# One decoder layer on one core: a product's two half-tiles closed in one step, a gated chunk turned two steps later

## The chip, the cores and the metric

The kernel runs on one core of a Trainium2 chip. The metric is the device time of one execution in microseconds (us), lower is better. Five engines work side by side, each through its own queue in order: TensorE (PE; PEld is its weight load), VectorE (DVE), ScalarE (ACT), GpSimd (POOL), and SyncE (SP), which here issues nearly all DMAs. An instruction that waits holds up all that stands behind it on its engine.

## The reference

One layer over 512 tokens of width 2048, all in float32:

```python
h = rms_norm(x, norm1_g)
qa, ka, va, ra, ga, qb, kb, vb = split(h @ w_in)        # combined projection
out_a = gla_mixer(qa, ka, va, ra, log_g(ga), onorm_g)   # gated linear attention, 4 heads
                                                        # ends with rms_norm(o) * silu(ra)
out_b = dilated_mixer(rms(qb), rms(kb), vb, rel_bias)   # 8 heads
x = x + concat(out_a, out_b) @ w_out                    # "the output product"
h2 = rms_norm(x, norm2_g)
x = x + (silu(h2 @ w_gate) * (h2 @ w_up)) @ w_down      # hidden width 5632
```

## The kernel before

**Products.** Every large matrix product is done in pairs of 512 output columns by a seven-product scheme (`P1 P5 P6 P3 P7 P2 P4`) instead of eight block products. The activations are operands in `apool` (tiles `AA` for single blocks, `AS` for sums of blocks), the weights stream in as quarters `wa wb wc wd` of 512 KB. One *item* is one product times one of four row groups: ACT casts the weight tile to a high part `wh` (L320), DVE takes the low part `wl` (L324, and first a sum of two quarters at L230 where the product needs one), and PE runs 8 matmuls with `wh` and 4 with `wl` (L364). `stream` writes the items of all pairs out one after the other; `wh` and `wl` have two buffers each.

**Side work.** After the eighth matmul of each item `p.step()` runs. It counts down every entry of `later(units, fn)` by one and emits those that reach zero; so `later(2, ...)` means two items on. Then it emits some of the `background` jobs. All this is only the order of the program: a scheduler then sets each engine's own order from it, by its own costs, and places the waits.

**Closing.** Four products close an output chunk: `P3` closes (half 0, which 1), `P7` (1,1), `P2` (0,0), `P4` (1,0). `half` is a half of the tokens, `which` one of the pair's two chunks of 512 columns. `close` adds the product (two PSUM tiles `acc`, m = 0 and 1) to the two `seed` tiles on DVE, m = 0 one step after the product's end (L277), m = 1 two steps after it, and then calls `final`.

**The output product** is two pairs: columns 0 to 1023, then 1024 to 2047 (`final_out(1)`). There `final` adds the residual (`seed<-seed,q` and `seed<-seed,k`, L1445), stores the rows to `x_d`, sums their squares (ACT L1478), scales them (ACT L1453, tile `L`), and two steps later PE turns them by 8 transposes (L1166, `bank<-mats,L`); ACT copies the banks out (L1177, tiles `oT` and `PT`) and SP stores them to `xn_d`, from where the operands of the feed-forward product are loaded. For (1,1) `final` also queues `early_jobs` and `late_jobs`: the first load both token halves of `xn_d[6]` and `xn_d[7]` into tiles `top` (L1227), cast them (ACT L178, DVE L179, `AA<-top`) and form the difference of the two halves (DVE L1265) with its cast `AS<-top`. The chunk closed by (1,1) is one of these halves.

**The gate rows.** The pair before the output product makes `r`; `final_gate` multiplies the attention output by silu(r), tile `cr` in its last call, which takes `P4`'s PSUM directly (`src is acc_`). `rest` (L1215) finishes the product and queues `transposed_store`, which turns the two tiles by 8 transposes (`bank<-mats,cr`), copies them out (ACT L1174, `turned`) and stores them to `mix_d`, from where later `late_jobs` load them for the sums `late<-oT,late` (DVE L1300). Tiles called `C`, which hold `seed` and `cr`, have six buffers; PSUM tiles `bank` have four.

Of the kernel before, what the change touches and what calls it, by code (L numbers as in the profile page):

```python
# [31 lines left out]
PRODUCTS = ("P1", "P5", "P6", "P3", "P7", "P2", "P4")  # L32
# [76 lines left out]
def block_kernel(ctx: ExitStack, tc: tile.TileContext, ins, out):  # L109
# [19 lines left out]
    def nm(s):  # L129
        uid[0] += 1  # L130
        return f"{s}_{uid[0]}"
# [4 lines left out]
    def bank():  # L136
        return ps.tile([P, 512], F32, name=nm("bank"), tag="bank")

    def work(tag, shape=(P, 512), bufs=1):
        return mp.tile(list(shape), F32, name=nm(tag), tag=tag, bufs=bufs)  # L140
# [25 lines left out]
    class Operand:  # L166


        def __init__(self, groups):
            self.groups = groups  # L170
            self.t = {}
# [20 lines left out]
    def unfolded(t):  # L192

        return t.rearrange("p (a b) -> p b a", b=2)

    def halves(t):
        return t.rearrange("p (b a) -> p b a", b=2)

    class Pair:


        def __init__(
            self, op, rows, w1, w2, final, step, scale=None, before=None, products=PRODUCTS
        ):
            self.op, self.rows, self.w1, self.w2 = op, rows, w1, w2
            self.final, self.step, self.scale, self.before = final, step, scale, before
            self.q, self.dst, self.held = {}, {}, {}
            self.products = products
            self.closes = {**CLOSES}
            if products is FIRST_CLOSED:  # L210
                self.closes["P1"] = self.closes.pop("P2")
# [62 lines left out]
        def close(self, seed, src, half, which):  # L274
            def one(m):
                if self.scale is None:
                    nc.vector.tensor_tensor(  # L277
                        halves(seed[m]), unfolded(src[m]), halves(seed[m]), op=ALU.add
                    )
                else:  # L280
                    nc.vector.scalar_tensor_tensor(  # L281
                        halves(seed[m]), unfolded(src[m]), self.scale(half, m), halves(seed[m]),
                        op0=ALU.mult, op1=ALU.add,
                    )
                if m == 1:
                    self.final(half, which, seed, None)

            later(1, lambda: one(0))
            later(2, lambda: one(1))

        def end(self, prod):
            src = self.dst[prod]
# [84 lines left out]
    def soon(fn, groups=1):  # L377

        soonest.append([groups, fn])
# [123 lines left out]
    def later(units, fn, hold=False):  # L503

        deferred.append([units, fn, hold])
# [49 lines left out]
    def rate(*stretches):  # L555


        owed = [0.0]
        rates = iter([r for n, r in stretches for _ in range(n)])

        def go():
            owed[0] += next(rates, stretches[-1][1])
            n = owed[0] if owed[0] > 0.3 else 0
            owed[0] = min(owed[0] - (step(n) or 0.0), 1.0)

        return go
# [592 lines left out]
    def transposed_store(tiles, half, dsts, gains=None, spare=None):  # L1159

        for b in range(2):
            bk = bank().rearrange("p (j n) -> p j n", j=2)
            for jj in range(2):
                for m in range(2):
                    f = (2 * b + jj) * P
                    nc.tensor.transpose(  # L1166
                        bk[:, jj, m * P : (m + 1) * P], tiles[m][:, f : f + P], ident
                    )
            if spare is None:
                d = work(("oT", "PT")[b], (P, 2, 256))  # L1170
            else:
                d = spare[:, b]
            if gains is None:
                nc.scalar.copy(d, bk)  # L1174
            else:
                for jj in range(2):
                    nc.scalar.activation(  # L1177
                        d[:, jj, :], bk[:, jj, :], AF.Copy,
                        scale=gains[:, 2 * b + jj : 2 * b + jj + 1],
                    )  # L1180
            store(dsts[b][:, :, half * 256 : (half + 1) * 256], d)
            done.add((id(dsts[b]), half))
# [9 lines left out]
    def final_gate(half, which, tiles, acc_):  # L1192
        og = onorm.pop((half, which))
        if tiles is None:
            tiles = [cpool.tile([P, 512], F32, name=nm("cr"), tag="C") for _ in range(2)]
            src = acc_
        else:
            src = tiles
        for m in range(2):
            if src is acc_:  # L1200
                nc.vector.scalar_tensor_tensor(
                    halves(og[m]), unfolded(src[m]), row_scale(half, m), halves(og[m]),
                    op0=ALU.mult, op1=ALU.mult,
                )
                neg = nrs1[:, 2 * half + m : 2 * half + m + 1]
                nc.scalar.activation(halves(tiles[m]), unfolded(src[m]), AF.Exp, scale=neg)
            else:
                nc.vector.tensor_tensor(og[m], src[m], og[m], op=ALU.mult)
                nc.scalar.activation(tiles[m], src[m], AF.Exp, scale=-1.0)
            nc.scalar.activation(tiles[m], tiles[m], AF.Ln, bias=1.0)  # L1210
            nc.scalar.activation(tiles[m], tiles[m], AF.Exp, scale=-1.0)

        def rest():
            for m in range(2):
                nc.vector.tensor_tensor(tiles[m], tiles[m], og[m], op=ALU.mult)  # L1215
            spare = apool.tile([P, 2, 2, 256], F32, name=nm("turned"), tag="A")
            later(3 - (src is acc_), lambda: transposed_store(
                tiles, half, mix_d[2 * which : 2 * which + 2], spare=spare
            ))

        soon(rest, 2)
# [174 lines left out]
    opm = Operand(4)  # L1396
# [5 lines left out]
    def pair(*args, **kw):  # L1402
        pairs.append(Pair(*args, **kw))

    pair(opx, rows_in, col(1536), col(1024), final_proj("va1", "va0"), rate((22, 1), (6, 0.6)),
         row_scale, before=lambda: background.extend([gates(), bias_tables()]))
# [5 lines left out]
         products=FIRST_CLOSED)  # L1412


    rows_mix = [(1024 + 256 * g, 256 * order[g]) for g in range(4)]
# [41 lines left out]
    def final_out(second):  # L1457
        rest_of = {}

        def ahead(half, which):  # L1460
            tok = 1 - half
            rest_of[half, which] = residual_loads(
                [2 * tok, 2 * tok + 1], 512 * (2 * second + which),
                lambda t, c: x[t * P : (t + 1) * P, c : c + 512],
                "C" if (half, which) == (1, 0) else "qk",
            )

        def final(half, which, tiles, acc_):
            tok = 1 - half
            rows = [2 * tok, 2 * tok + 1]  # L1470
            ch = 2 * second + which
            last = tiles is None
            tiles = residual(tiles, acc_, rest_of.pop((half, which)))
            for m in range(2):
                t = rows[m]
                store(x1_d[t][:, 512 * ch : 512 * ch + 512], tiles[m])
                jk = work("st", (P, DV), bufs=2).bitcast(mybir.dt.bfloat16)
                nc.scalar.activation(  # L1478
                    jk, tiles[m], AF.Square, accum_out=ss2[:, t, ch : ch + 1]
                )  # L1480
            if second:
                def scaled():
                    turn = scaled_store(tiles, rows, tok, xn_d[2 * ch : 2 * ch + 2], 4 * ch)
                    later(2, turn)

                if last:
                    later(4, scaled)
                else:
                    scaled()
                if which == 1 and half == 1:  # L1490
                    background.append(early_jobs(opn, (2, 3), tops, False))
                    background.append(late_jobs(opn, ((2, 3),), tops, bots, False))
                if which == 0 and half == 1:
                    output_scales()
            elif which == 0 and half == 1:
                nc.vector.tensor_tensor(part2, ss2[:, :, 0], ss2[:, :, 1], op=ALU.add)
                first_scale()
                background.append(first_columns())
                background.append(operand_jobs(opn, (0, 1), tops, bots))

        final.ahead = ahead
        return final
# [41 lines left out]
    ocol = lambda c: w_out[:, c : c + 512]  # L1544
# [10 lines left out]
    tops = [xn_d[2], xn_d[3], xn_d[6], xn_d[7]]  # L1555
    bots = [xn_d[0], xn_d[1], xn_d[4], xn_d[5]]
    pair(opm, rows_mix, ocol(0), ocol(512), final_out(0), paced([1] * 28))
    pair(opm, rows_mix, ocol(1024), ocol(1536), final_out(1), rate((28, 1.2)))


    rows_n = [(512, 0), (768, 256), (1536, 1024), (1792, 1280)]
# [165 lines left out]
    for i in range(3):  # L1727
        g0 = 4 * i
        rows_d = [(512 * (g0 + g), 512 * (g0 + g) + 256) for g in range(opd[i].groups)]
        for np_ in range(2):  # L1730
# [5 lines left out]
                before=(lambda i=i: background.append(down_jobs(i + 1))) if lead else None,  # L1736
# [46 lines left out]
```

## Time and profile before

| | us |
|---|---|
| median of 3 runs (lowest, highest) | 1935.62 (1932.67, 1936.36) |
| the profiled execution | 1928.62 |
| its span, first to last instruction | 1926.8 |
| PE busy in it | 1900.7 |
| DVE busy in it | 1684.6 |

The profiled execution is 7.0 us shorter than the median, 1.8 us of it lie outside the span. In the profile's rows "idle" in square brackets is the time the engine stood just before the instruction, and the name behind the arrow is what ended it.

### The profile page before, as it was taken

Reading aid. Unit: us, or ns where it says so; the run is one execution under the profiler, and the core shown is the slowest. Engines: PE = TensorE matmul, PEld = TensorE weight load, DVE = VectorE, ACT = ScalarE, POOL = GpSimd, SP = SyncE. Lnnn points to the kernel's source line nnn. Section 1 sums busy time; section 2 is a strip of 40 time slices with the busy share of each in tenths; the row PEclk is TensorE's granted clock in tenths of the full one; section 3 lists DMA queues with packets and bytes.
Section 4 is the critical chain, followed back from the end, with each engine's and each line's share of the span. In section 5 each row is a group of like instructions: output and inputs, shape, how many; then the busy total and the mean of one; then the engine's idle time right before and its main releaser. Section 6 shows DMA issues by size and latency. Waiting matters only on the chain.

```text
span 1926.8 us, 25472 instructions
## 1 busy us (share of the span) xinstructions
PE 1900.7 (99%) x8986; PEld 1642.7 (85%) x8986; DVE 1684.6 (87%) x1915; ACT 1070.6 (56%) x1550; POOL 58.0 (3%) x80
## 2 busy tenths in 40 slices
PE   8999999999999999999999999999999999999999
PEld 7888888888888878888888888888888888888887
DVE  8997887877999799978878879879879989989987
ACT  8564564567776676544544444544446546546543
POOL 1000221010000010000000000000000000000000
PEclk9999999999999999999999999999999999999999
DMA  8458365476767594564564554564556785955761
GB/s 284 132 167 277 102 190 153 137 209 196 221 228 245 188 310 158 154 191 147 154 191 144 151 186 132 158 190 123 166 184 188 215 283 175 277 205 173 247 219 66
DMA packets 341800, 362.01 MB, mean 188 GB/s; under 512 B 132790, under 2 KB 202623, under 8 KB 341672
## 3 DMA queue, kind: packets, MB, share of 16 engines
q1 hardware_dynamic: 341320, 360.17, 59.6%
q8 instruction: 70, 1.15, 0.2%
q14 instruction: 58, 0.48, 0.1%
q10 hardware_dynamic: 352, 0.21, 0.0%
HBM read 298.16 MB, written 64.51 MB: 188 GB/s over the span
## 4 chain that ended last, share of the span: by engine, by line
PE 68%; DVE 11%; issue 3%; DMA 3%; ACT 1%; POOL 0%; DVEq 0%; SPq 0%; ACTq 0%; POOLq 0%
PE acc L364 66%; DVE wl L324 5%; DVE wa L230 2%; DVE AS L179 1%; PE bank L1033 1%; PE bank L999 1%; DVE wb L230 1%; ACT wh L320 0%; DVE AA L179 0%; DMA wc<-in_w_gate 0%; PE bank L1026 0%; DVE seed L281 0%; DMA top<-xn_d 0%; DMA r<-xn_d 0%; DMA x_d<-seed 0%
## 5 line engine op out<-in xcount | busy, mean ns | idle before, releaser
L364 PE MATMUL acc<-wh,AS 128*128 128x512 f32 x3008 | 710.9, 379 | 0.0
L364 PEld LDWEIGHTS acc<-wh,AS 128*128 128x128 f32 x3008 | 568.3, 189 | 81.1 <-issue 0.2
L320 ACT CAST wh<-wa 128x1024 fp32r<-128x1024 f32 x376 | 394.0, 1049 | 400.3 <-PE acc L364 369.7
L364 PE MATMUL acc<-wh,AA 128*128 128x512 f32 x2256 | 535.8, 380 | 2.1 <-ACT wh L320 1.8
L324 DVE TENSOR_TENSOR wl<-wa,wh 128x1024 fp32r<-128x1024 f32 x376 | 456.8, 1217 | 53.0 <-ACT wh L320 46.1
L364 PEld LDWEIGHTS acc<-wh,AA 128*128 128x128 f32 x2256 | 426.8, 189 | 64.6 <-ACT wh L320 3.3
L364 PE MATMUL acc<-wl,AS 128*128 128x512 f32 x1504 | 398.0, 386 | 7.3 <-DVE wl L324 7.1
L364 PEld LDWEIGHTS acc<-wl,AS 128*128 128x128 f32 x1504 | 279.5, 189 | 60.5 <-DVE wl L324 20.0
L364 PE MATMUL acc<-wl,AA 128*128 128x512 f32 x1128 | 295.1, 384 | 1.7 <-DVE wl L324 1.5
L364 PEld LDWEIGHTS acc<-wl,AA 128*128 128x128 f32 x1128 | 211.3, 189 | 36.4 <-DVE wl L324 6.4
L320 ACT CAST wh<-wb 128x1024 fp32r<-128x1024 f32 x94 | 98.6, 1048 | 125.3 <-PE acc L364 108.5
L320 ACT CAST wh<-wc 128x1024 fp32r<-128x1024 f32 x94 | 98.4, 1047 | 113.1 <-PE acc L364 108.7
L230 DVE TENSOR_TENSOR wa<-wc,wa 128x1024 f32<-128x1024 f32 x94 | 114.5, 1222 | 49.6 <-DMA wc<-in_w_gate 30.1
L320 ACT CAST wh<-wd 128x1024 fp32r<-128x1024 f32 x94 | 98.5, 1048 | 99.1 <-PE acc L364 96.9
L324 DVE TENSOR_TENSOR wl<-wc,wh 128x1024 fp32r<-128x1024 f32 x94 | 114.6, 1219 | 35.8 <-ACT wh L320 34.3
L324 DVE TENSOR_TENSOR wl<-wd,wh 128x1024 fp32r<-128x1024 f32 x94 | 114.4, 1220 | 16.2 <-ACT wh L320 11.9
L324 DVE TENSOR_TENSOR wl<-wb,wh 128x1024 fp32r<-128x1024 f32 x94 | 113.6, 1217 | 6.7 <-ACT wh L320 6.5
L230 DVE TENSOR_TENSOR wa<-wb,wa 128x1024 f32<-128x1024 f32 x94 | 113.5, 1219 | 2.0 <-DMA wb<-in_w_down 1.1
L230 DVE TENSOR_TENSOR wb<-wd,wb 128x1024 f32<-128x1024 f32 x94 | 114.6, 1219 | 0.6
L230 DVE TENSOR_TENSOR wa<-wd,wa 128x1024 f32<-128x1024 f32 x94 | 112.9, 1219 | 0.0
L281 DVE SCALAR_TENSOR_TENSOR seed<-acc,rs,seed 128x512 f32<-128x512 f32 x96 | 70.5, 746 | 23.3 <-PE acc L364 23.3
L265 ACT ACTIVATE seed<-acc,rs 128x512 f32<-128x512 f32 x96 | 60.6, 680 | 0.8 <-PE acc L364 0.8
(309 smaller groups left out, 1313.2 us busy)
## 6 DMA issues: line engine op xcount, KB each, us to landing
wa<-in_w_gate SPq DMA_DIRECT2D x44, 512.0 KB, 3.8
wb<-in_w_up SPq DMA_DIRECT2D x44, 512.0 KB, 4.5
wd<-in_w_up SPq DMA_DIRECT2D x44, 512.0 KB, 3.5
wc<-in_w_gate SPq DMA_DIRECT2D x44, 512.0 KB, 3.4
wc<-in_w_in SPq DMA_DIRECT2D x32, 512.0 KB, 4.1
wa<-in_w_in SPq DMA_DIRECT2D x24, 512.0 KB, 5.8
wb<-in_w_in SPq DMA_DIRECT2D x24, 512.0 KB, 5.7
wd<-in_w_in SPq DMA_DIRECT2D x24, 512.0 KB, 6.5
```

Source lines behind the costliest of these rows:

```text
L179: nc.vector.tensor_tensor(low, src, high.bitcast(F32), op=ALU.subtract)
L230: nc.vector.tensor_tensor(src, minuend, src, op=ALU.subtract)
L265: nc.scalar.activation(halves(t), unfolded(src[m]), AF.Copy, scale=self.scale(half, m))
L281: nc.vector.scalar_tensor_tensor(halves(seed[m]), unfolded(src[m]), self.scale(half, m), halves(seed[m]), op0=ALU.mult, op1=ALU.add,)
L320: nc.scalar.copy(high[k], sources[k])
L324: nc.vector.tensor_tensor(low[k], sources.pop(k), high[k].bitcast(F32), op=ALU.subtract)
L364: nc.tensor.matmul(p.dst[prod][m], a[:, jj, hl, m * P : (m + 1) * P], folded(w[:, jj, :]), start=fresh and g == 0 and len(terms) == 2 and ...
L999: nc.tensor.matmul(lp[:, :n], qh[:, b * P : (b + 1) * P], kh[:, :n], start=True, stop=True)
L1033: nc.tensor.matmul(op, vh[:, k, :], lgs[b][:, k * P : (k + 1) * P], start=(k == 0), stop=(k == b))
```

## The change

Two edits. `Pair` takes a list `at_once` of (half, which); for those `close` emits the second half-tile, and with it `final`, in the same step as the first. The second output pair gets `at_once=((1, 1),)`, so what `P7` closes there comes one step earlier. And in `final_gate` the turning of the last chunk, the one that is taken from PSUM, is queued 4 steps on instead of 2; the other chunks stay at 3.

```diff
         def __init__(
-            self, op, rows, w1, w2, final, step, scale=None, before=None, products=PRODUCTS
+            self, op, rows, w1, w2, final, step, scale=None, before=None, products=PRODUCTS,
+            at_once=(),
         ):
...
-            self.products = products
+            self.products, self.at_once = products, at_once
...
             later(1, lambda: one(0))
-            later(2, lambda: one(1))
+            later(1 if (half, which) in self.at_once else 2, lambda: one(1))
...
             spare = apool.tile([P, 2, 2, 256], F32, name=nm("turned"), tag="A")
-            later(3 - (src is acc_), lambda: transposed_store(
+            later(3 + (src is acc_), lambda: transposed_store(
                 tiles, half, mix_d[2 * which : 2 * which + 2], spare=spare
             ))
...
-    pair(opm, rows_mix, ocol(1024), ocol(1536), final_out(1), rate((28, 1.2)))
+    pair(opm, rows_mix, ocol(1024), ocol(1536), final_out(1), rate((28, 1.2)),
+         at_once=((1, 1),))
```

## The prediction

> **What bounds the kernel now.** I read the page's busy times first, then PE's waits along the whole trace, then a table of windows over the two places that the diff touches, then the queues there row by row.
>
> ```profile
> PE 1900.7 (99%) x8986; PEld 1642.7 (85%) x8986; DVE 1684.6 (87%) x1915; ACT 1070.6 (56%) x1550; POOL 58.0 (3%) x80
> 540.00:560.00 20.00, 18.83 (x104) 16.40 (x103) 19.87 (x26) 17.25 (x28) 0.00 (x0) 1.00 0.78 268
> 560.00:580.00 20.00, 19.36 (x89) 16.33 (x88) 20.00 (x24) 13.05 (x19) 0.00 (x0) 1.00 0.37 120
> 580.00:600.00 20.00, 20.00 (x94) 17.50 (x94) 20.00 (x24) 13.23 (x19) 0.00 (x0) 1.00 0.46 159
> 710.00:720.00 10.00, 8.08 (x30) 6.27 (x29) 7.17 (x12) 7.27 (x14) 3.19 (x3) 0.84 0.95 302
> 720.00:740.00 20.00, 18.65 (x89) 15.84 (x88) 20.00 (x24) 13.64 (x20) 2.89 (x3) 0.99 0.46 156
> PE acc L364 <- DVE wl L324: 3.2, 7, 1.2
> ```
>
> PE is busy for 1900.7 of 1926.8 us, so an edit can win only in the places where PE stands. The last row is all that PE waits from 741 us to the end: 3.2 us, none of it near the edits. What either edit changes before 741 us is carried to the end, since PE is the bound there. The gate rows are turned at 557 us and the output's third chunk is closed at 686 to 720 us. In both places the third column from the left (DVE) reads 19.87 to 20.00 of 20 us, except in 710 to 720, where it is 7.17 of 10. There alone something can be won, and by DVE: before and after it DVE sets PE's pace.
>
> **First edit: the gate rows turned two steps later.**
>
> ```profile
> 557.23 0.41 PE L1166 MATMUL bank<-mats,cr 128*128 128x128 f32 x2 [1.17 <-DVE cr L1215]
> 579.73 1.13 PE L364 MATMUL acc<-wl,AS 128*128 128x512 f32 x4 [0.62 <-DVE wl L324]
> 576.12 0.68 DVE L1300 TENSOR_TENSOR late<-oT,late 128x512 f32<-128x512 f32 x1
> 560.14 1.22 SPq L1181 DMA_DIRECT2D mix_d<-turned  x2
> ```
>
> PE stands 1.17 us before the first of 8 transposes, for `cr`. In the compiled order of the changed kernel seven of them stand about 4 us later, behind the first item of P5, but one stays in front of the last item of P1 and still waits for the same `cr`, some 0.65 us. Then PE runs into the next `wl` earlier and waits there for the rest, for DVE has no idle time in this stretch (19.87, 20.00, 20.00 above) and has the same instructions to do; only four of them change places among themselves. The wait of 0.62 us at 579.73, for `wl`, stays at its time. Gain: 0, at most 0.1 us either way; if DVE were not full, it would be the 1.17 us. The two stores to `mix_d` move from 560.1 to about 564.2 on SP, and the loads of `oT` and `PT` behind them wait for them. The store and the load take at most 6.8 us each by the row on landings below, so `oT` is there before 578, more likely by 571. DVE wants it at 576.12. I take no cost; the bound is 2 us.
>
> **Second edit: the chunk of P7 closed in one step.** The rows of before, by engine: the closing, the PE stop it leads to, and DVE.
>
> ```profile
> 688.43 0.68 DVE L179 TENSOR_TENSOR AS<-r,AS 128x512 fp32r<-128x512 f32 x1
> 690.90 0.68 DVE L277 TENSOR_TENSOR seed<-acc,seed 128x512 f32<-128x512 f32 x1
> 692.10 0.69 DVE L1445 TENSOR_TENSOR seed<-seed,k 128x512 f32<-128x512 f32 x1
> 693.46 1.32 ACT L1453 ACTIVATE L<-seed,prox 128x512 f32<-128x512 f32 x2
> 694.83 0.98 PE L1166 MATMUL bank<-mats,L 128*128 128x128 f32 x7 [0.28 <-ACT L L1453]
> 698.95 0.52 SPq L1181 DMA_DIRECT2D xn_d<-PT  x1
> 699.56 1.37 SPq L185 DMA_DIRECT2D wd<-in_w_up  x2
> ...
> 703.99 0.68 DVE L1445 TENSOR_TENSOR seed<-seed,k 128x512 f32<-128x512 f32 x1
> 704.79 0.57 SPq L1281 DMA_DIRECT2D T<-xn_d  x1
> 707.87 1.18 SPq L1227 DMA_DIRECT2D top<-xn_d  x2
> ...
> 709.82 1.28 DVE L1442 TENSOR_TENSOR rows<-acc,rows 128x512 f32<-128x512 f32 x2
> 711.06 1.23 DVE L324 TENSOR_TENSOR wl<-wa,wh 128x1024 fp32r<-128x1024 f32 x1
> 714.37 0.62 ACT L178 CAST AA<-top 128x512 fp32r<-128x512 f32 x1 [2.10 <-DMA top<-xn_d]
> 715.12 0.69 DVE L1265 TENSOR_TENSOR top<-top 128x512 f32<-128x512 f32 x1 [2.83 <-DMA top<-xn_d]
> 715.98 3.64 PE L364 MATMUL acc<-wh,AA 128*128 128x512 f32 x8 [1.84 <-ACT wh L320]
> 719.42 1.45 PE L364 MATMUL acc<-wl,AA 128*128 128x512 f32 x4
> 720.71 1.89 PE L364 MATMUL acc<-wh,AA 128*128 128x512 f32 x8
> 722.44 1.03 PE L364 MATMUL acc<-wl,AA 128*128 128x512 f32 x4
> 721.09 0.68 DVE L1296 TENSOR_TENSOR r<-qT,r 128x512 f32<-128x512 f32 x1
> 732.86 1.13 PE L364 MATMUL acc<-wl,AS 128*128 128x512 f32 x4 [0.95 <-DVE wl L324]
> DMA to landing us min/median/max: 3.0/5.2/6.8
> ```
>
> The stop: both ACT and DVE wait for `top`, the loads of `xn_d[6]`. They are issued at 707.87 and 708.44, because SP stands from 700.93 to 704.79 before `T<-xn_d`, which needs the store issued at 698.95 to land; ACT's cast of the next weight tile is queued behind `AA<-top`, so PE stops for 1.84 us, and DVE idles 2.83 us. The last row is the landing time of DMAs that touch `xn_d` between 680 and 740 us.
>
> Closing: the second L277 moves from 690.90 to right behind the DVE rows of 688.4, that is to 689.0; both L1445 are done by 690.9 (692.8 before). ACT squares and scales until 693.2 (before 693.46 + 1.32 = 694.8). PE's transposes stand one item earlier in the compiled order, so PE waits for the scaled rows from 691.6 to 693.25 instead of 0.28 us; by item P4.0 it is 1.0 us late. ACT copies out at 695.1, and the store that was issued at 698.95 goes out at 696.65, 2.3 us earlier. `T` follows at its old distance, 704.79 - 698.95 = 5.8 us, at 702.5. The cover for PE's 1.0 us is the stop at 715.98: by P1.0 of the feed-forward product I have PE 0.4 us behind its old time, and then it waits for DVE anyway. If that cover is gone it costs 0.4 to 1.0 us.
>
> Loads: in the changed queue of SP both halves of `top` stand ahead of the next `xn_d` stores, but the second half stands behind two stores `x_d<-seed` that wait for P2's closing, whose last L1445 (703.99 before) I get at 704.75 to 705.4. So the second half is issued at 706.0 (before 708.44). It lands 3.0 to 6.8 us later: 709.0 to 712.8. I take 4.1 us, halfway from the least to the median 5.2, since one DMA fewer lies ahead of it than before: 710.1.
>
> DVE: L1265 moves ahead of both L1442 and of `wl` of P1.1, so a late `top` now holds up that `wl` too. From the first L1442 at 709.82 to the end of the stretch at 721.09 DVE does twelve instructions in 11.27 us, 2.83 of them idle and 0.1 small gaps: 8.3 us of work. The changed order has the same twelve. DVE comes to L1265 at 709.55 (the `wl` before it is about 0.3 us earlier, as two casts on ACT go before the squares). With no pause it ends the stretch at 709.55 + 8.3 = 717.9 instead of 721.1, a gain of 3.2 us; with `top` landing at 710.1 it pauses 0.55 us, and the gain is 2.6 us; with 712.8 it pauses 3.25 us, and nothing is won. ACT has to deliver the two casts of weight tiles in this stretch by 713.8 and 716.8; I get 713.7 and 716.4. After 721 DVE is full (20.00 of 20), and PE's waits of 0.95 at 732.86 and the like stay, all earlier by the gain.
>
> Sum: 0 + 2.6 = 2.6 us. The profiled execution of 1928.62 becomes 1926.0. It lies 7.0 us under the median of the runs, and the edits touch nothing that could explain that; so against the median 1935.62 - 2.6 = **1933.0**.
>
> [...] After the 1.84 us stop 8 matmuls took 3.64 us, where the same form took 1.89 at 720.71, and the granted clock reads 0.84 in 710 to 720; the 1.17 us stop at 557.23 left the clock at 1.00. So I count a wait of 1.84 us as dangerous and one of 1.2 as not, and the new wait of 1.65 us at 691.6 lies between. [...] The half clock's own price, (3.64 - 1.89) + (1.45 - 1.03) = 2.2 us, is not in my sum on either side, for DVE is the later of the two there.
>
> **The rivals.**
>
> *PE was the bound after all, and gains more.* Then the stop of 1.84, the half clock's 2.2 and the wait of 0.95 go: 5.0 us, 1930.6. For it: the clock was low for 3.4 us just there. Against: DVE at 20.00 of 20 from 720 on. Chance 0.24.
>
> *Nothing comes of it*: `top` lands at about 712.8 as its longest landing says, DVE's idle time only moves ahead of `wl`. 1935.6. For it: the DMA share is 0.95 there. Chance 0.06.
>
> *Slower: `top` before `wl` in DVE's queue.* It decides at 712.8: each microsecond later is lost whole, since `wl` of P1.1, both L1442 and, by the `rows`, ACT's casts now stand behind it. If the loads keep their old time, 708.44 + 6.5 = 715.0, the loss is 2.2 us; PE then stops for over 3 us, and with the half clock (2.2 us) and the wait of 1.0 us at 691.6 no longer covered it can come to 4 us: 1939.6. For it: SP waits twice more on the way. Against: the store that starts the row goes out 2.3 us earlier. Chance 0.22.
>
> **How the numbers follow.** A difference under 0.2% (3.9 us) can hardly be told from none: the three runs lie 3.7 us apart. The forecast has a chance of 0.48; its own bounds, 0 to 3.2 us, are within 0.2%, but the scatter puts a third of it on the far side: 0.16 faster, 0.32 same. The first rival is faster (0.24), the second same (0.06), of the third 0.18 slower and 0.04 same. Together 0.40, 0.42, 0.18. The range reaches from the first rival less half the scatter, 1930.6 - 1.9 = 1928.7, to the third's end, 1939.6; about 2 in 10 lie beyond these.
>
> **What would show it.** Right: DVE's idle time before L1265 under 1 us and L1265 ahead of L1442; the `bank<-mats,L` transposes of the third chunk near 693 with a PE wait of about 1.5 us; no PE stop near 714 and no clock under 1.00 in 700 to 740; the wait for `wl` at 579.7 as before. Wrong: `top` landing after 712.8, PE waits at 560 to 600 that are gone, or a time beyond 0.2% on either side.

## The result and the profile after

| | before | after |
|---|---|---|
| median us (lowest, highest), 10 runs each, taken side by side | 1935.49 (1932.67, 1937.54) | 1939.94 (1938.18, 1942.45) |
| the profiled execution | 1928.62 | 1939.63 |

The ratio is 1.0027 (1.0017 to 1.0037): slower by 4.5 us, where 2.6 us less was forecast. Lines of the changed kernel count one more than before's behind L203, and two more behind L1558. PE stood 0.94 us later at the matmul that starts at 684.96 us in before's trace; where I compare places in the second half of the trace I take that off.

PE's waits on its timeline, at the two places of the edits:

```profile
558.55 0.30 PE L1167 MATMUL bank<-mats,cr 128*128 128x128 f32 x1 [0.53 <-DVE cr L1216]
561.40 1.13 PE L365 MATMUL acc<-wl,AA 128*128 128x512 f32 x4 [0.35 <-DVE wl L325]
581.05 1.13 PE L365 MATMUL acc<-wl,AS 128*128 128x512 f32 x4 [0.62 <-DVE wl L325]
...
693.62 0.33 PE L1167 MATMUL bank<-mats,L 128*128 128x128 f32 x1 [0.89 <-ACT L L1454]
694.23 0.98 PE L1167 MATMUL bank<-mats,L 128*128 128x128 f32 x7 [0.28 <-ACT L L1454]
716.30 1.13 PE L365 MATMUL acc<-wl,AA 128*128 128x512 f32 x4 [1.69 <-DVE wl L325]
733.80 2.07 PE L365 MATMUL acc<-wl,AS 128*128 128x512 f32 x4 [4.91 <-DVE wl L325]
```

All but the last row are as forecast or as before: the wait for `cr` is parted into one for `cr` and one for `wl`, the transposes of the third chunk wait a little, the stop at 716 is still there, now for `wl` where before waited for `wh`. The last row is new: 4.91 us, where before waited 0.40 at the same matmuls:

```profile
728.18 1.13 PE L364 MATMUL acc<-wl,AS 128*128 128x512 f32 x4 [0.40 <-DVE wl L324]
```

The windows say the same (columns: length, then busy time of PE, PEld, DVE, ACT and POOL, the granted clock, the DMA share and GB/s):

```profile
710.00:720.00 10.00, 8.30 (x33) 6.47 (x32) 6.76 (x12) 7.04 (x16) 0.00 (x0) 0.90 1.00 327
720.00:740.00 20.00, 15.09 (x60) 12.48 (x60) 15.50 (x18) 9.01 (x14) 9.82 (x5) 0.80 0.21 77
```

In 720 to 740 DVE has 15.50 of 20 us where it had 20.00, the clock is 0.80 instead of 0.99, and POOL has 9.82 us for five instructions where the same five took 6.1 (3.19 and 2.89 in the prediction's rows). So the question is what those five are, and who waits for them. The rows of the timeline there that bear on it:

```profile
719.77 0.16 DVE L1549 TENSOR_TENSOR tmp<-tmp,part 128x4 f32<-128x4 f32 x1
720.02 7.45 POOL L159 TENSOR_SCALAR rs<-tmp 128x4 f32<-128x4 f32 x1 [269.06 <-DVE tmp L1549]
726.19 1.23 DVE L231 TENSOR_TENSOR wa<-wb,wa 128x1024 f32<-128x1024 f32 x1
727.55 0.19 POOL L1551 TENSOR_SCALAR part<-part 128x4 f32<-128x4 f32 x1
727.82 1.01 POOL L160 TENSOR_TENSOR rs<-rs,mhalf 128x4 f32<-128x4 f32 x1
728.79 1.01 POOL L1552 TENSOR_TENSOR part<-part,phalf 128x4 f32<-128x4 f32 x1
729.88 0.20 POOL L1553 TENSOR_TENSOR rs<-rs,part 128x4 f32<-128x4 f32 x1
730.11 1.26 ACT L266 ACTIVATE seed<-acc,rs 128x512 f32<-128x512 f32 x2 [5.01 <-POOL rs L1553]
731.92 0.69 DVE L179 TENSOR_TENSOR AS<-r,AS 128x512 fp32r<-128x512 f32 x1 [4.50 <-ACT AS L178]
```

and the same work in before:

```profile
716.65 1.10 POOL L159 TENSOR_SCALAR rs<-tmp 128x4 f32<-128x4 f32 x1 [266.69 <-DVE tmp L1548]
717.62 1.22 DVE L324 TENSOR_TENSOR wl<-wa,wh 128x1024 fp32r<-128x1024 f32 x1
717.83 1.06 POOL L1550 TENSOR_SCALAR part<-part 128x4 f32<-128x4 f32 x1
718.96 1.34 POOL L160 TENSOR_TENSOR rs<-rs,mhalf 128x4 f32<-128x4 f32 x1
720.27 1.76 POOL L1551 TENSOR_TENSOR part<-part,phalf 128x4 f32<-128x4 f32 x1
722.12 0.85 POOL L1552 TENSOR_TENSOR rs<-rs,part 128x4 f32<-128x4 f32 x1
723.97 1.26 ACT L265 ACTIVATE seed<-acc,rs 128x512 f32<-128x512 f32 x2
```

These are `output_scales`: when the last output chunk is closed, two small DVE additions make `tmp` and five GpSimd operations on 128x4 numbers make `rs`, one scale per token. ACT needs `rs` for the first seeds of the feed-forward product. Before, `rs` was ready at 722.97, 1.0 us ahead of ACT. After, the first of the five lasted 7.45 us, to 727.47; DVE had gone idle at 727.42, for its next cast waits for ACT, which waits for `rs`. PE at the end of that chain stood 4.91 us and then ran at half clock (granted 0.50 from 734 to 738 us; its next 8 matmuls with `wh` took 3.24 us, the same 8 in before 1.89).

And the gain? The queue of SP up to `top`:

```profile
697.55 0.52 SPq L1182 DMA_DIRECT2D xn_d<-PT  x1
698.16 0.57 SPq L185 DMA_DIRECT2D wb<-in_w_up  x1
698.82 0.60 SPq L185 DMA_DIRECT2D wd<-in_w_up  x1
705.10 0.57 SPq L1282 DMA_DIRECT2D T<-xn_d  x1
706.42 0.57 SPq L1228 DMA_DIRECT2D top<-xn_d  x1
708.16 2.38 SPq L1228 DMA_DIRECT2D top<-xn_d  x3
...
713.82 0.69 DVE L1266 TENSOR_TENSOR top<-top 128x512 f32<-128x512 f32 x1 [3.24 <-DMA top<-xn_d]
722.12 0.69 DVE L1297 TENSOR_TENSOR r<-qT,r 128x512 f32<-128x512 f32 x1
```

The DMA view of 690 to 706 us (packets, MB, share of 16 engines' time), after and then before:

```profile
q1 hardware_dynamic: 3464, 5.56, 95.2%
q1 hardware_dynamic: 3680, 5.96, 99.2%
```

The store goes out 2.3 us earlier (697.55 - 0.94 against 698.95), but `T` follows it by 7.55 us, not by 5.84. The second half of `top`, the first of the three loads at 708.16, lets DVE's L1266 start 5.7 us later, at 713.8 - 0.9 = 712.9: the point from which nothing is won. The stretch of twelve instructions ends at 722.12 - 0.94 = 721.2, before at 721.09. The DMA engines were full in both kernels, so their share alone does not tell 7.55 from 5.84; what else was under way is looked at below.

### The profile page after: what moved, and what is told of

The parts are those of the page before. It is cut to its first block, busy times and chain, and to the rows that moved or that the text cites. A ratio compares the mean times of both kernels' runs of the same rounds, so it can differ in the third digit from the quotient of the medians.

```text
span 1937.8 us, 25475 instructions
## 1 busy us (share of the span) xinstructions
PE 1905.9 (98%) x8986; PEld 1645.1 (85%) x8986; DVE 1684.5 (87%) x1915; ACT 1069.8 (55%) x1550; POOL 62.2 (3%) x80
## 4 chain that ended last, share of the span: by engine, by line
PE 78%; DVE 11%; DMA 4%; issue 4%; ACT 2%; POOL 1%; SPq 0%; DVEq 0%; POOLq 0%; ACTq 0%
PE acc L365 70%; DVE wl L325 5%; PE acc L433 3%; DVE wa L231 2%; DMA wc<-in_w_gate 1%; DVE AS L179 1%; PE bank L1034 1%; PE bank L1000 1%; ACT wh L321 1%; DVE wb L231 1%; DVE AA L179 0%; DMA wd<-in_w_up 0%; PE bank L786 0%; POOL rs L159 0%; PE bank L1167 0%
## 5 line engine op out<-in xcount | busy, mean ns | idle before, releaser
L231 DVE TENSOR_TENSOR wa<-wc,wa 128x1024 f32<-128x1024 f32 x94 | 114.7, 1225 | 54.9 <-DMA wc<-in_w_gate 33.3
L231 DVE TENSOR_TENSOR wb<-wd,wb 128x1024 f32<-128x1024 f32 x94 | 115.1, 1225 | 0.6
L231 DVE TENSOR_TENSOR wa<-wb,wa 128x1024 f32<-128x1024 f32 x94 | 113.6, 1221 | 1.9 <-DMA wb<-in_w_down 1.0
L231 DVE TENSOR_TENSOR wa<-wd,wa 128x1024 f32<-128x1024 f32 x94 | 113.2, 1223 | 0.0
```

The source lines that it names most:

```text
L231: nc.vector.tensor_tensor(src, minuend, src, op=ALU.subtract)
```

## The experiments

A yardstick for all of them: PE's time from the matmul that starts at 684.96 us in before's trace to the one at 740.96, looked up in each trace (after: 685.90 to 747.39, 61.5 us), and from there to the end of the span. Each ratio is to runs of before timed beside the kernel; their median was 1929.77 us beside e9 to e12 and 1934.3 to 1935.5 beside the others.

| kernel | 685 to 741 | rest | first GpSimd operation | ratio to before |
|---|---|---|---|---|
| before; again (e1) | 56.0; 56.1 | 1185.9; 1189.4 | 1.10; 1.10 | 1 |
| after; again (e7) | 61.5; 61.5 | 1190.5; 1190.5 | 7.45; 7.45 | 1.0027; 1.0018 (1.0007 to 1.0028) |
| e2, first edit | 56.1 | 1194.4 | 1.10 | 0.9997 (0.9989 to 1.0006) |
| e3, second edit | 60.3 | 1188.5 | 7.45 | 1.0022 (1.0013 to 1.0031) |
| e4, after, scales off GpSimd | 55.6 | 1194.5 | none | 1.0013 (1.0005 to 1.0022) |
| e5, before, scales off GpSimd | 56.5 | 1190.8 | none | 1.0020 (1.0011 to 1.0028) |
| e6, after, DVE holds | 56.4 | 1188.4 | 1.10 | 0.9996 (0.9987 to 1.0004) |
| e8, e4 with top's way clear | 55.5 | 1189.9 | none | 1.0011 (1.0002 to 1.0020) |
| e9, e6 with top first | 52.7 | 1186.5 | 1.10 | 0.9987 (0.9978 to 0.9996) |
| e10, before, DVE holds | 55.7 | 1186.9 | 1.10 | 1.0000 (0.9991 to 1.0008) |
| e11, before, scales a step later | 60.8 | 1186.1 | 7.51 | 1.0027 (1.0017 to 1.0038) |
| e12, after, scales a step later | 60.8 | 1186.1 | 7.45 | 1.0026 (1.0017 to 1.0036) |
| f1, before, DVE holds, top first | 54.3 | 1190.4 | 1.10 | 0.9994 (0.9985 to 1.0002) |
| f2, after, copy from PSUM | 61.4 | 1192.9 | 0.19, then 8.31 | 1.0026 (1.0013 to 1.0039) |
| f3, after, copy from SBUF | 59.9 | 1191.3 | 7.78 | 1.0026 (1.0016 to 1.0036) |

The first column parts the kernels in two: 59.9 to 61.5 where GpSimd was kept out for over 7 us, at most 56.5 elsewhere, with either closing. The second spreads over 8.7 us and goes with neither; e9 to e12, which were timed beside the same runs of before, lie within 0.8 us of each other.

**e1 and e7: both kernels again.**

> The kernel before, unchanged, for a second profile: the profiled execution of before (1928.62) lay 7.0 us under the median of its own runs, that of after (1939.63) on its median. Theory (GpSimd's five small operations in output_scales, which took 1.10, 1.06, 1.34, 1.76 and 0.85 us in the first profile of before and 7.45, 0.19, 1.01, 1.01 and 0.20 in that of after, are slowed by chance as much as by the change): the second profile lies near 1935 and shows the first of the five, at 716 us, several microseconds long, with ScalarE waiting for it at 724 us. Rival (the change alone brings the long one): all five again under 2 us and no wait on ScalarE; then the 7 us lie elsewhere.

> The changed kernel, unchanged, beside the others for a second profile and a second timing. Theory: 1.0027 again (1.0017 to 1.0037); GpSimd's first operation 7.45 us, ScalarE's wait about 5 us; from 741 us to the end PE loses between 0 and 8.5 us against the first profile of before, as the profiles of all kernels do, by the gate's weights landing late (0, 3.6, 8.5, 4.6, 2.6 and 8.6 us so far). Rival (the changed kernel's own loss there): 4 us or more again in that part while a kernel without the change shows less.

The theory of e1 fell: before's five GpSimd operations are the same to 0.01 us in the second profile, those of after too. It is no scatter. Before's first profile has the shortest rest of all the traces, 3.6 us shorter than its second.

**e2 and e3: one edit each.** In e2 only `later(3 + (src is acc_), ...)` is changed, in e3 only `at_once`.

> The first edit alone: the gate rows turned two steps later, the third chunk closed in two steps as before. Theory (the loss comes from the second edit): ratio 1.000, within 0.0015, about 1935.5 us; the PE waits at 557 us split into two of together 0.9 to 1.2 us and the first of GpSimd's five operations in output_scales under 2 us. Rival (the first edit costs, through the stores to mix_d and the loads behind them): 1.002 to 1.003 with new waits between 560 and 600 us.

> The second edit alone: the third chunk closed in one step, the gate rows turned when they were before. Theory (the whole loss is the second edit's): ratio 1.0027, 1.0017 to 1.0037, about 1940 us; GpSimd's first operation in output_scales near 720 us lasts 5 us or more, ScalarE waits over 3 us for the scales and PE about 5 us for wl of the feed-forward product. Rival (the two edits only lose together, or the first one loses): 1.000 to 1.001 and no long GpSimd operation.

e2: 0.9997, with the two rows at 557:

```profile
557.43 0.30 PE L1166 MATMUL bank<-mats,cr 128*128 128x128 f32 x1 [0.52 <-DVE cr L1215]
560.28 1.13 PE L364 MATMUL acc<-wl,AA 128*128 128x512 f32 x4 [0.35 <-DVE wl L324]
```

e3: 1.0022, GpSimd 7.45 us. The loss is the second edit's.

**e4 and e5: the scales without GpSimd**, on the changed kernel and on before.

```diff
-        rsqrt_mean(rs2, tmp2, D)
-        nc.gpsimd.tensor_scalar(part2, part2, 2.0 / D, EPS, op0=ALU.mult, op1=ALU.add)
-        nc.gpsimd.tensor_tensor(part2, part2, phalf, op=ALU.pow)
-        nc.gpsimd.tensor_tensor(rs2, rs2, part2, op=ALU.mult)
+        nc.vector.tensor_scalar(tmp2, tmp2, 1.0 / D, EPS, op0=ALU.mult, op1=ALU.add)
+        nc.scalar.activation(rs0, tmp2, AF.Ln)
+        nc.scalar.activation(rs0, rs0, AF.Exp, scale=-0.5)
+        later(1, refine)  # three DVE steps, then rs2 *= root, with root = xms * prox made in first_scale
```

> The changed kernel with the token scales of output_scales worked out without GpSimd: the root of the mean on ScalarE by logarithm and exponential, one refining step on VectorE, and the product with the old scale's root from a factor made ahead. It adds five small VectorE operations (0.07 us each by the two that are there) and two on ScalarE. Theory (ScalarE's wait of 5.01 us for GpSimd's last operation is the loss): that wait is gone, PE's wait of 4.91 us for wl near 729 us is gone with its half clock of 3.4 us, and the time falls by 4.5 to 8 us from 1940, to 1932 to 1935.5, ratio 0.998 to 1.000. Rival (the loss is the late load of top and the half clock at 717 us, and GpSimd only takes time in which others would wait anyway): 1938 to 1940, ratio 1.0015 to 1.0025.

> The kernel before with the token scales worked out without GpSimd, as in the run of the changed kernel: the control for it. That run came to 1.0013 (1.0005 to 1.0022), so some 2.5 us of the loss remain or come from the edit itself. Theory (before, the five GpSimd operations were done 1 us ahead of ScalarE, so taking them away saves nothing, and the seven small operations cost 0.07 us each on VectorE, 0.4 us, and nothing else): 1.000, 0.9993 to 1.0007. Rival (the edit costs by itself, through VectorE's queue standing behind ScalarE's logarithm): 1.001 to 1.002, and the changed kernel loses nothing besides GpSimd.

In e4 the wait of 4.91 us is gone and the stage is back at 55.6 us, but the time is only 1.0013, between the two ranges expected. e5 says why that can't be read as a rest of the loss: the substitution alone costs before 1.0020. In the stage it costs 0.5 us at most. All three kernels that have it reach 685 us late (687.7, 688.3, 689.8 against 683.7 to 687.5 of the others), ahead of nearly all that it changes. Where that comes from stays open.

**e6 and e10: GpSimd keeps its work, DVE stands still for the first operation.**

```diff
-        rsqrt_mean(rs2, tmp2, D)
+        nc.gpsimd.tensor_scalar(rs2, tmp2, 1.0 / D, EPS, op0=ALU.mult, op1=ALU.add)
+        nc.vector.tensor_copy(tmp2, rs2)
+        nc.gpsimd.tensor_tensor(rs2, tmp2, mhalf[:, :4], op=ALU.pow)
```

> The changed kernel, all five GpSimd operations kept; one VectorE copy of 128x4 is put behind the first of them and reads its result, so VectorE has to stand still until that operation is through. Theory (GpSimd's first operation lasted 7.45 us because VectorE's instructions followed one another without a gap; it ended 0.05 us after VectorE fell idle): with VectorE standing it takes 0.2 to 1.2 us, VectorE idles about as long, the scales are ready by 727 us, ScalarE's wait falls from 5.01 us to under 1.5 and PE's of 4.91 for wl to about 1; 1934.5 to 1937.5 us. Rival (the operation is slow by itself after 269 us in which GpSimd stood): it again takes 7 us or more, VectorE idles as long in the middle of the stretch, and the time is 1941 us or more.

> The kernel before with VectorE held for GpSimd's first operation: the control. Theory (before, GpSimd got in between VectorE's instructions within 1.1 us and the scales were ready 1 us ahead of ScalarE; nothing was lost there, and holding VectorE costs 0.2 us): 1.000, 0.9993 to 1.0008. Rival (holding VectorE wins for another reason): 0.998 to 0.999.

e6's timeline:

```profile
719.75 1.23 DVE L231 TENSOR_TENSOR wa<-wb,wa 128x1024 f32<-128x1024 f32 x1
719.94 1.10 POOL L1550 TENSOR_SCALAR rs<-tmp 128x4 f32<-128x4 f32 x1 [269.09 <-DVE tmp L1549]
721.07 0.17 DVE L1551 COPY tmp<-rs 128x4 f32<-128x4 f32 x1
725.06 0.85 POOL L1555 TENSOR_TENSOR rs<-rs,part 128x4 f32<-128x4 f32 x1
725.95 1.26 ACT L266 ACTIVATE seed<-acc,rs 128x512 f32<-128x512 f32 x2 [0.67 <-POOL rs L1555]
```

The operation ends at 721.04, 0.06 us after DVE's L231, and not at 727. The four behind it got in without a hold, at 1.9 us or less each. That the operation would be slow by itself after a long pause is refuted; it had idled 269 us here too. Against the changed kernel's 1.0027 and 1.0018 this is 0.9996: a DVE gap of about 0.1 us takes the whole loss away. In before the same hold changes nothing (1.0000).

**e11 and e12: the scales one step later**, `later(1, output_scales)` for `output_scales()`, in before and in after.

> The kernel before with output_scales called one step later, so that the same five GpSimd operations start beside other VectorE instructions, some 3.5 us later. Theory (whether GpSimd gets in depends on where it meets VectorE's row, and the edit only moved that place): the first operation may last anything from 1 to 8 us; if it lasts 4 us or more, ScalarE waits as in the changed kernel and the time is 1.002 to 1.003 with neither edit made; if it lasts 1 to 2 us the scales still come 2 to 3 us behind ScalarE and the time is 1.0005 to 1.0015. Rival (only the changed kernel's own row keeps GpSimd out): 1 to 2 us in any case.

> The changed kernel with output_scales called one step later. Theory (the place decides): the first operation starts near 722.5 us instead of 720 and either still ends only when VectorE falls idle (1.003 or more, since VectorE falls idle when ScalarE waits for the scales) or gets in at once, and then the scales come 1 to 3 us late: 1.0005 to 1.002. Rival (GpSimd always loses against this row): ends when VectorE falls idle, near 727.5 us, 1.0025.

```profile
717.50 7.51 POOL L159 TENSOR_SCALAR rs<-tmp 128x4 f32<-128x4 f32 x1 [267.79 <-DVE tmp L1548]
727.67 1.27 ACT L265 ACTIVATE seed<-acc,rs 128x512 f32<-128x512 f32 x2 [5.02 <-POOL rs L1552]
```

This is e11: neither edit is in it, and it has the long operation, ACT's wait of 5.02 us and the full loss, 1.0027. In DVE's row only the two `tmp` stand elsewhere: the last one behind `wa` and `wl` and ahead of `AS`, where before had it ahead of `wa`. In e12 the scheduler left the two `tmp` where they were, between the same neighbours as in after, so it tells nothing new.

**f2 and f3: what keeps GpSimd out.** One DVE copy of 128x512 is queued right behind `tmp`; it waits for nothing of GpSimd's. In f2 it reads PSUM, in f3 SBUF.

```diff
+                    with tc.issue_after(behind):  # the last tmp
+                        nc.vector.tensor_copy(jk, acc_[1])   # f3: tiles[1]
```

> The changed kernel with one VectorE copy of 128x512 from PSUM to SBUF (half precision, its result unused) queued right behind tmp, so that GpSimd's first operation meets one instruction of some 0.65 us that has no SBUF input; VectorE does not wait for GpSimd. Theory (only VectorE's operations with two SBUF inputs keep GpSimd out): the operation gets in beside the copy or at its end and lasts under 1.2 us, the rest are through by 727 us, ScalarE waits under 1.5 us; 0.999 to 1.001. Rival (VectorE must stand still; any instruction keeps GpSimd out): it ends when VectorE falls idle, near 728 us, and the time is 1.002 to 1.0035.

> As the copy from PSUM, but the copy of 128x512 reads SBUF, one input. Theory (operations with two SBUF inputs keep GpSimd out, with one they do not): as for the copy from PSUM, under 1.2 us and 0.999 to 1.001. Rivals: a copy from SBUF keeps GpSimd out where one from PSUM does not (7 us here, 1 us there), or both do (1.002 to 1.0035).

f2, then f3:

```profile
719.42 0.69 DVE L1498 CAST st<-acc 128x512 bf16<-128x512 f32 x1
719.61 0.19 POOL L159 TENSOR_SCALAR rs<-tmp 128x4 f32<-128x4 f32 x1 [269.34 <-DVE tmp L1552]
719.88 0.19 POOL L1554 TENSOR_SCALAR part<-part 128x4 f32<-128x4 f32 x1
720.02 1.23 DVE L231 TENSOR_TENSOR wa<-wb,wa 128x1024 f32<-128x1024 f32 x1
720.15 8.31 POOL L160 TENSOR_TENSOR rs<-rs,mhalf 128x4 f32<-128x4 f32 x1
```

```profile
717.45 0.42 DVE L1498 CAST st<-rows 128x512 bf16<-128x512 f32 x1
717.63 7.78 POOL L159 TENSOR_SCALAR rs<-tmp 128x4 f32<-128x4 f32 x1 [267.39 <-DVE tmp L1552]
```

Beside the copy from PSUM two GpSimd operations take 0.19 us each; the third meets L231 with its two SBUF inputs and lasts 8.31 us. So the operation got in beside this copy, as the theory of f2 said, and the time did not follow: the block only moved to the third operation, 1.0026. The copy from SBUF let nothing in, though it has one input and lasts 0.42 us, less than the one from PSUM: the operation started 0.16 us ahead of L231 (717.79) and lasted 7.78 us, where f2's second one started 0.14 us ahead of it and lasted 0.19. That only VectorE's operations with two SBUF inputs keep GpSimd out, the theory of both, is refuted.

What keeps GpSimd out is shown here only by its times. In before the first operation ended 0.13 us behind the next DVE boundary (717.75 against 717.62); in after it was passed over at seven boundaries, from 720.98 to 726.19. What let it in at the first boundary in before is not shown by any run, and stays open; the two places have the same pair of DVE instructions, `wa` and then `wl`. Nor is it shown what sets the two copies apart: they differ in source, PSUM and SBUF, and in length, 0.69 and 0.42 us.

**e8, e9, f1: the way of `top`.** The four stores `x_d<-seed` of the chunks closed at P7 and P2, and three weight loads, are issued behind the loads of `top`; in e9 and f1 also the loads of `qT`, `kT`, `v` and `T`. e8 stands on e4, e9 on e6; f1 is before with e9's hold and queue.

```diff
-                store(x1_d[t][:, 512 * ch : 512 * ch + 512], tiles[m])
+                puts.append(lambda t=t, r=tiles[m]: store(x1_d[t][:, 512 * ch : 512 * ch + 512], r))
...
+            with tc.issue_after(tops_seen[0]):  # the last load of top; so too for the loads
+                while puts:
+                    puts.pop(0)()
```

> The changed kernel without GpSimd in the scales, and with the way of top made free: the four stores x_d<-seed of the chunks closed at P7 and P2, and three of the weight loads (512 KB each), are queued on SP behind the loads of top. Theory (T and top came late because the DMA engines were full, 95% of 690 to 706 us, so that the earlier store landed no earlier: 7.5 us from issue to T instead of 5.8; and the second half of top stood behind two stores that waited for P2): with 0.5 MB less ahead of T and 1 MB less beside it, T goes out 1.5 to 3 us earlier, both halves of top by 705.5, they land by 710.5, VectorE's wait before L1266 falls from 3.2 us to under 1 and PE's near 716 from 1.7 to under 0.5, without half clock; 2 to 4 us less than the same kernel without this, 1933.5 to 1936. Rival (the transfer takes its 7 us whatever else is under way): T at 704 to 705 as now, 1937 to 1938.

> The changed kernel with VectorE held for GpSimd's first operation, and with top's four loads first behind the store of the third chunk: the four x_d stores, the loads of qT, kT, v and T, and three weight loads queue behind them on SP. In the run that freed top's way without this, T went out 3.6 us earlier against PE's time, 3.95 us behind the store instead of 7.5, but then v stood 2.5 us ahead of top, waiting for its buffer, and top won only a part. Theory (the forecast's gain of 2.6 us was right in mechanism, and failed only because the store and the loads had to share a full DMA): top lands by 709.5 against PE's time of before, VectorE's wait before L1266 falls under 1 us, and the time is 2 to 3 us below the run with VectorE held (0.9996): 0.998 to 0.9988. Rival (VectorE's work from there to 735 us sets the pace anyway, or what is now late elsewhere eats it): 0.999 to 1.000.

> The kernel before (closing in two steps) with VectorE held for GpSimd's first operation and top's loads first in SP's queue, as in the run of the changed kernel that came to 0.9987 (0.9978 to 0.9996). Theory (the closing in one step brings the store 2.3 us forward, and with the queue free of other transfers top with it): here top lands some 2 us later against PE's time, VectorE waits 1 to 2.5 us before L1265, and the time is 0.9993 to 1.0005. Rival (the queue alone wins, the closing nothing): 0.998 to 0.999 here as well.

SP's queue in e8, then in e9, with a row of DVE in e9:

```profile
701.45 0.52 SPq L1189 DMA_DIRECT2D xn_d<-PT  x1
705.40 0.57 SPq L1302 DMA_DIRECT2D T<-xn_d  x1
708.51 0.57 SPq L1302 DMA_DIRECT2D v<-xn_d  x1
709.17 2.53 SPq L1237 DMA_DIRECT2D top<-xn_d  x4
```

```profile
699.17 0.52 SPq L1189 DMA_DIRECT2D xn_d<-PT  x1
702.54 2.53 SPq L1237 DMA_DIRECT2D top<-xn_d  x4
710.28 0.68 DVE L1286 TENSOR_TENSOR top<-top 128x512 f32<-128x512 f32 x1
```

With less beside it (a DMA share of 88.3% in 690 to 706 us in both, 95.2% in after) the store is through 3.95 us after its issue in e8 and 3.4 in e9, instead of 7.55: its landing hangs on what else is under way. In e8 `v` came ahead of `top`, waiting for its buffer, and took the gain back (1.0011 against e4's 1.0013). In e9 DVE does not wait for `top` at all, PE has no stop at 716 and a granted clock of 1.00 from 710 to 740 us, the stage takes 52.7 us, 3.3 less than before, and the kernel beats both: 0.9987 (0.9978 to 0.9996). The theory of f1 fell: with the closing in two steps and the queue cleared DVE does not wait at L1265 either, and the stage is 54.3. So the queue alone wins 1.4 of e9's 3.0 us against e10 (55.7); the rest is what the closing in one step adds, in one profile each; in f1's a wait of 0.84 us of DVE for `qT`, whose load was put behind `top`, is part of it. The times, 0.9987 and 0.9994, do not separate the two.

## Why the prediction was wrong

Step by step.

*First edit, 0.* Right, and for its reason: one transpose stayed in front with 0.53 us of wait (0.65 forecast), 0.35 us came back as a wait for `wl`, and the wait of 0.62 stayed. PE in after was 1.31 us behind before at the matmul of 550.42 and 1.32 at that of 582.42, so nothing was won, and e2 is 0.9997. The cover over the stores to `mix_d` held.

*Closing.* Right: `x_d` and squares in time, PE's wait before the transposes 0.89 + 0.28 = 1.17 us instead of 1.65, the clock 1.00, the store 2.3 us earlier.

*"`T` follows at its old distance, 5.8 us".* This step failed first. The distance was not the store's own: 7.55 us here and 5.7 to 7.6 in all the traces with the closing in one step and the old queue (e4 6.80, e6 7.25, e7 7.30), 5.0 to 5.9 in those with two steps (e5 5.61, before 5.84), 3.95 and 3.4 in e8 and e9, where less was under way. `T` went out 0.6 us earlier instead of 2.3, the second half of `top` at 708.16 - 0.94 = 707.2 instead of 706.0, and `top` came at 712.9, just where the forecast had its point of no gain.

*"I take 4.1 us, halfway from the least to the median".* This term was too small as well: the second half took 5.7 us from its issue to L1266. Of the 2.8 us by which `top` missed 710.1, 1.2 are the late issue and 1.6 the landing. e3 shows the second alone: there the half went out at 706.84 - 0.82 = 706.0, as forecast (0.82 us is e3's lag at 685 us), and L1266 started at 713.36, 6.5 us later. Together the two steps bring about the rival "nothing comes of it" (0.06), a gain of 0; the loss comes from elsewhere.

*The sum over "the same twelve instructions".* It counted DVE's own time right (the stretch ended 0.1 us from its old place), but asked only who waits for DVE's 128x512 and 128x1024 rows. The two `tmp` among them moved as well, from 715.73 and 716.41, near the head of the row, to 719.10 and 719.77 near its end, and with them the start of five GpSimd operations. GpSimd's 3.19 and 2.89 us of busy time stood in the quoted windows, and ACT's wait for `rs` had a margin of 1.0 us; the prediction named neither. This is the whole of the loss: e6 gives the price, 4.2 us between its median and e7's, taken side by side (1933.73 and 1937.92), and 5.1 in the stage (56.4 and 61.5), and e11 shows it without the edit.

*The rival "PE was the bound after all".* After could not test it, for `top` was late. In e9, where DVE does not wait for `top`, the stage won 3.0 us against e10 and 3.3 against before: near the 3.2 that the sum gave to DVE without a pause, and not the rival's 5.0.

*The rival "slower".* Its time, up to 1939.6, was near and its mechanism was not the one: `top` did not come after 712.8 by more than 0.1 us.

*"The edits touch nothing that could explain" the 7.0 us.* Right as far as it is shown: of the 4.9 us between the spans of before's two profiles (1926.8 and 1931.7 us) 3.6 lie in the rest, and neither trace has an edit in it.

## What to carry to other kernels

Before an edit shifts a full VectorE row, list the small GpSimd operations that start from it and who waits for the last of them, and how many tenths of a microsecond are to spare: a row of VectorE instructions without a gap, reading two SBUF operands each, held an operation for as long as the row lasted, 7.45 us in after, that took 0.19 us in f2. With one tiny instruction that made VectorE wait for the result, that operation took 1.10 us in e6, e9, e10 and f1; the later ones took up to 1.88 us there, but in f2, which lacks that instruction, it was the third that lasted 8.31. And a DMA's time from issue to landing, read in a stretch where the DMA engines are full, is not a distance that moves with the DMA (5.84 us from the store to `T` in before, 7.55 in after at 99.2% and 95.2% of the DMA engines' time): ask first what else would have to go.

## What was not expected of the hardware

In these traces each of GpSimd's five operations lasted either under 1.9 us or over 7, nothing between: 0.85 to 1.76 us in before, and the first of them 7.45 us in after, e3, e7 and e12, 7.51 in e11 and 7.78 in f3, and the third 8.31 in f2. VectorE had gone idle 0.04 to 0.06 us before the long one's end in after, e7, e11, e12 and f3, and 0.86 us before it in f2.

A PE stop alone does not say whether the clock is halved. In before the clock was half for 3.4 us, from 716.9 to 720.3 us, at the stop of 1.84 us. In after the stop of 1.69 us was followed by 8 matmuls in 3.35 us, at a granted clock of 0.50 from 717.9 to 721.3, in f2 one of 1.73 by 8 in 2.00. Around its stop of 4.91 us after's granted clock was half for 6.8 us, from 731.6 us, 2.2 us before PE went on, to 738.4, which adds to the price of the wait.

The same kernel's last 1185 us changed from 1185.9 to 1189.4 us between two profiles (e1), with PE's waits for `wl` there 3.2 and 4.5 us, where VectorE waits for the gate's weights: 30.1 and 34.7 us in all.
